# Normalised turned input of a hybrid GLA and S5 block: its tokens begin 192 bytes beyond a multiple of 256 bytes

## Chip, cores and metric

The kernel runs on one core of a Trainium2 chip. The metric is the device time of one execution in microseconds (us). The engines are named as in the profile: PE is TensorE's matrix multiplication, PEld its loading of weights, DVE is VectorE, ACT is ScalarE, POOL is GpSimd and SP is SyncE.

## The reference, cut to what matters

One decoder block is computed for 512 tokens of width 1024, with 16 meta tokens ahead of them (528 tokens in all):

```python
h = jnp.concatenate([meta, x], axis=1)          # 16 + 512 tokens
xn = rmsnorm(h, g_mix_pre)
proj = xn @ w_in                                # 1024 -> 6160 columns
# q, k, v, r, a_low, u, z_gla, z_ssm are slices of proj
y_gla = (rmsnorm(gla_chunked(q, k, v, log_a)) * silu(r)) @ w_o_gla
glu   = gelu(s5_ssm(u)) @ w_glu + b_glu
y_ssm = glu[..., :D] * sigmoid(glu[..., D:])
mixed = sigmoid(z_gla) * y_gla + sigmoid(z_ssm) * y_ssm
h = h + rmsnorm(mixed @ w_out, g_mix_post)
h = h + rmsnorm(square(relu(rmsnorm(h, g_ffn_pre) @ w_ff1)) @ w_ff2, g_ffn_post)
```

The change concerns `xn`, the operand of `xn @ w_in`.

## The kernel before

**The turned input.** `xn` is held turned: features on the 128 partitions, tokens along the free dimension, in eight feature tiles (`KT` = 8). It is held twice, as two float32r tensors that add up to it: `xh` (the rounded part, written by ScalarE in `high`, line 571) and `xl` (the rest, written by VectorE in `low`, line 576). The order along a row is the 512 tokens first and the 16 meta tokens last, `NT` = 528 numbers. The tensors are made with longer rows, `LINE + SEQ` = 64 + 512 = 576 numbers (2304 bytes, nine times 256), of which the first 528 are used (line 254).

**The products.** Each weight of `w_in` comes in tiles of 128 columns. A tile is loaded by SP (`wraw`, line 170), and split into a rounded part `whi` by ScalarE (lines 164 and 174) and a rest `wlo` by VectorE (line 179). `feat_tile` and `mm3` (lines 190 to 202) then make, for each of the eight feature tiles, three matmuls with a stationary tile of 128 x 128 and `xh` or `xl` as the moving operand:

```python
190 def mm3(ps, whi, wlo, xhi, xlo, kt, within=None):
...
195     PE.matmul(ps, whi(k), xhi(k), start=(k == 0), stop=False)
196     PE.matmul(ps, whi(k), xlo(k), start=False, stop=False)
197     last = PE.matmul(ps, wlo(k), xhi(k), start=False, stop=(k == kt - 1))
```

In the profile these are the rows `mm<-xh,whi`, `mm<-xl,whi` and `mm<-xh,wlo` of line 61, a helper that issues every matmul. A group of 24 of them makes one product. Where the meta tokens are wanted (u, v and k) a product is made in two halves, `HALVES = ((0, 256), (256, NT))`, so with moving operands of 256 and then 272 columns: three tiles of u (`u_half`, line 278), eight of v (`Head.value`, line 959) and four of k (`Head.key`, line 1010), together 15 groups of 24 of each width. Where they are not wanted (q, r and both gates z) a product takes the 512 tokens at once: four of q (line 1020), eight of r (line 1241) and sixteen of z (line 784), 28 groups of 24. The low-rank gate projection (`low_rank`, line 693) uses `xh` and `xl` with narrow weights `wa`: 32 matmuls, 32 or 16 weight columns each, half with 256 and half with 272 moving columns.

**The first tiles of u.** The first five of the eight tiles of u are made before the normalisation is known, from the raw input, in the same split form: `rh` and `rl`, with rows of the same 576 numbers of which the first 528 are used (line 462). Their matmuls have the same shapes and weights of the same kind as those of `xh` and `xl`; `raw_product` (line 582) makes them in the order of `mm3`, and `side_by_side` (line 586) makes two tiles in turn.

**Where the operands lie.** Most pools are padded: each tile takes a multiple of 256 bytes per partition (`mk`, lines 81 to 93). In the built program `xh` begins at byte 55040 of each partition and `xl` at 73472, both multiples of 256, and the `whi` and `wlo` buffers begin at multiples of 256 too. `rh` begins at 122048 and `rl` at 140480, 192 bytes beyond a multiple, since a pool that is not padded lies below theirs. With rows of 2304 bytes every feature tile of a tensor begins at the same place against 256, and the second half, 1024 bytes further on, as well.

**Order of work.** The program's order on PE, DVE and ACT is that of the code in this part (`keep_in_program_order`, lines 59 to 79; for DVE and ACT from line 521 to 1332). The products of `xh` and `xl` run from 38 us (the low-rank projection) to 350 us: u and seven tiles of z, then the heads of the GLA with the blocks of the S5 scan between the products, then the rest of z and r. Between the products stand float32 matmuls and transposes of these two parts. After 350 us neither tensor is read.

Of the kernel before, what the change touches and what calls it, by code (L numbers as in the profile page):

```python
# [10 lines left out]
F32R = mybir.dt.float32r  # L11
# [6 lines left out]
P = 128  # L18
D = 1024
KT = D // P  # L20
SEQ = 512
NM = 16
NT = NM + SEQ
# [8 lines left out]
LINE = 64  # L32
# [18 lines left out]
def hybrid_block(ctx: ExitStack, tc: tile.TileContext, io, out: bass.AP):  # L51
# [29 lines left out]
    def mk(pool, shape, dt=F32, tag=None, **kw):  # L81
        count[0] += 1
        name = f"{tag or 'x'}_{count[0]}"
        size = 1
        for n in shape[1:]:
            size *= n
        if pool not in lined or size % LINE == 0:
            return pool.tile(shape, dt, tag=tag or name, name=name, **kw)
        t = pool.tile([shape[0], -(-size // LINE) * LINE], dt, tag=tag or name, name=name, **kw)[:, :size]
        if len(shape) == 2:  # L90
            return t
        dims = " ".join("abcd"[: len(shape) - 1])
        return t.rearrange(f"p ({dims}) -> p {dims}", **dict(zip("abcd", shape[1:])))
# [4 lines left out]
    def pool(name, bufs=1, space=None, stack=None, side="left", padded=False):  # L98
        kw = {"side": side} if space is None else {"space": space}
        if space != DRAM:  # L100
            kw["reuse_waits"] = "tile"
        made = (stack or ctx).enter_context(tc.tile_pool(name=name, bufs=bufs, **kw))
        if padded:
            lined.append(made)
        return made
# [145 lines left out]
    s1 = ExitStack()  # L251
    px = pool("px", stack=s1, padded=True)
    pinned[0] = True
    xh, xl = (mk(px, [P, KT, LINE + SEQ], F32R, tag=t)[:, :, :NT] for t in ("xh", "xl"))
    w_in = io["w_in"][0]
    sg = ExitStack()
    pg = pool("pg", stack=sg)
# [1239 lines left out]
    for c4, c in enumerate(range(0, D, 256)):  # L1497
# [16 lines left out]
        for i, w in enumerate(load_w(wg[:, c : c + 256])):  # L1514
# [3 lines left out]
            t = mk(pgl, [P, SEQ], tag="ti", bufs=2)  # L1518
# [498 lines left out]
```

## Time and profile before

| | before |
|---|---|
| median of 3 runs | 869.69 us (869.55 to 870.79) |
| the profiled execution | 869.07 us, of which the span is 867.3 us |
| PE busy | 854.4 us (99%), 4952 matmuls |
| PEld busy | 727.7 us (84%) |
| DVE, ACT, POOL busy | 683.9 us (79%), 466.5 us (54%), 151.5 us (17%) |
| granted TensorE clock | 0.998 of full speed |

The span reaches from the first to the last instruction. A matmul's duration in the profile runs from its start to the end of its pipeline, so that one overlaps the next; what a matmul costs in a row of them is the time from its start to the next one's start, called its spacing here. It is read from the timeline, which gives starts to 0.01 us: from the first start of a row of n matmuls to the start of what follows, divided by n.

### The profile page before, as it was taken

The numbers are of one execution on the slowest core, as the hardware profiler recorded it, in microseconds if no ns is written. First come the engines' busy times: TensorE is split into PE (matmuls) and PEld (weight loads), VectorE is DVE, ScalarE is ACT, GpSimd is POOL, SyncE is SP. The second block draws the span as 40 slices with busy tenths as digits, with TensorE's granted clock in tenths as the row PEclk, the third lists the DMA queues.
The fourth block names the chain that finished last, engine by engine and source line by source line (L and its number), as shares of the span: only waits on it lengthen the run. The fifth ranks groups of instructions, "written<-read, shape, count | busy, mean of one in ns | idle before, by whom it ended". The sixth has DMA issues, their size and how long they took to land.

```text
span 867.3 us, 13744 instructions
## 1 busy us (share of the span) xinstructions
PE 854.4 (99%) x4952; PEld 727.7 (84%) x4952; DVE 683.9 (79%) x1263; ACT 466.5 (54%) x818; POOL 151.5 (17%) x265
## 2 busy tenths in 40 slices
PE   9999999999999999999999999999999999999996
PEld 7998889898988888888888888988888888888885
DVE  6999889979687699866888778576676677688886
ACT  7677466666764554335454466333222236885763
POOL 1123021130304223251121421021121100000001
PEclk9999999999999999999999999999999999999999
DMA  9887766655556757668788895488989967866564
GB/s 314 208 260 229 216 141 159 174 133 147 131 139 170 242 131 209 215 177 288 220 267 268 267 297 168 153 305 289 360 264 341 348 241 225 278 198 198 166 206 145
DMA packets 172492, 192.66 MB, mean 222 GB/s; under 512 B 18649, under 2 KB 127353, under 8 KB 172425
## 3 DMA queue, kind: packets, MB, share of 16 engines
q1 hardware_dynamic: 145040, 109.66, 44.1%
q0 software_dynamic: 25408, 77.93, 26.9%
q10 hardware_dynamic: 1976, 4.20, 1.7%
q8 instruction: 39, 0.64, 0.3%
q14 instruction: 29, 0.23, 0.1%
HBM read 149.52 MB, written 42.24 MB: 221 GB/s over the span
## 4 chain that ended last, share of the span: by engine, by line
PE 87%; DVE 7%; DMA 3%; ACT 2%; issue 1%; ACTq 0%; DVEq 0%; SPq 0%
PE mm L61 64%; PE sm L61 22%; DMA wraw<-in_w_ff_dram 2%; PE sm L66 1%; DMA wraw<-in_w_in_dram 1%; DVE aq L79 1%; DVE wlo L179 1%; DVE wlo L79 1%; DVE M L79 0%; ACT L79 0%; DVE bl L79 0%; DVE aq L1431 0%; DVE c L1937 0%; ACT hh L79 0%; DVE xT L79 0%
## 5 line engine op out<-in xcount | busy, mean ns | idle before, releaser
L164 ACT ACTIVATE whi<-wraw 128x1024 fp32r<-128x1024 f32 x81 | 85.8, 1060 | 182.2 <-PE mm L61 170.4
L179 DVE TENSOR_TENSOR wlo<-wraw,whi 128x1024 fp32r<-128x1024 f32 x81 | 98.9, 1222 | 77.2 <-ACT whi L164 77.1
L61 PE MATMUL mm<-xh,whi 128*128 128x512 f32 (+2 forms) x464 | 158.9, 342 | 0.0
L61 PE MATMUL mm<-xh,wlo 128*128 128x512 f32 (+2 forms) x464 | 155.9, 336 | 0.0
L61 PE MATMUL mm<-xl,whi 128*128 128x512 f32 (+2 forms) x464 | 155.6, 335 | 0.0
L61 PE MATMUL mm<-hl,whi 128*128 128x512 f32 (+1 forms) x272 | 100.8, 371 | 0.3 <-DVE hl L79 0.3
L61 PE MATMUL mm<-hh,whi 128*128 128x512 f32 (+1 forms) x272 | 100.8, 371 | 0.0
L61 PE MATMUL mm<-hh,wlo 128*128 128x512 f32 (+1 forms) x272 | 100.7, 370 | 0.0
L61 PEld LDWEIGHTS mm<-xh,whi 128*128 128x128 f32 x464 | 87.6, 189 | 9.7 <-issue 1.0
L61 PEld LDWEIGHTS mm<-xh,wlo 128*128 128x128 f32 x464 | 87.5, 189 | 9.0
L61 PEld LDWEIGHTS mm<-xl,whi 128*128 128x128 f32 x464 | 87.7, 189 | 8.4
L1854 DVE TENSOR_TENSOR wlo<-wraw,whi 128x1024 fp32r<-128x1024 f32 x56 | 68.4, 1222 | 21.9 <-ACT whi L1850 21.8
L61 PE MATMUL sm<-wlo,fh 128*128 128x512 f32 x192 | 74.8, 390 | 0.0
L61 PE MATMUL sm<-whi,fl 128*128 128x512 f32 x192 | 74.7, 389 | 0.0
L61 PE MATMUL sm<-whi,fh 128*128 128x512 f32 x192 | 74.7, 389 | 0.0
L1850 ACT ACTIVATE whi<-wraw 128x1024 fp32r<-128x1024 f32 x56 | 58.7, 1049 | 16.4 <-PE mm L61 11.7
L61 PEld LDWEIGHTS mm<-hl,whi 128*128 128x128 f32 x272 | 51.3, 188 | 9.3 <-DVE hl L79 0.6
L61 PEld LDWEIGHTS mm<-hh,whi 128*128 128x128 f32 x272 | 51.2, 188 | 8.8
L61 PEld LDWEIGHTS mm<-hh,wlo 128*128 128x128 f32 x272 | 51.2, 188 | 8.7
L164 ACT ACTIVATE fh<-f 128x512 fp32r<-128x512 f32 x48 | 30.2, 630 | 36.6 <-PE sm L61 22.8
L61 PE MATMUL mm<-gh,whi 128*128 128x512 f32 x128 | 49.8, 389 | 0.0
L61 PE MATMUL mm<-gl,whi 128*128 128x512 f32 x128 | 49.8, 389 | 0.0
(490 smaller groups left out, 1858.8 us busy)
## 6 DMA issues: line engine op xcount, KB each, us to landing
wraw<-in_w_ff_dram SPq DMA_DIRECT2D x56, 512.0 KB, 7.3
wraw<-in_w_in_dram SPq DMA_DIRECT2D x46, 512.0 KB, 4.4
w2raw<-in_w_ff_dram POOLq DMA_DIRECT2D x16, 1024.0 KB, 9.1
t2d<-w2t POOLq DMA_DIRECT2D x16, 1024.0 KB, 6.2
wraw<-t2d SPq DMA_DIRECT2D x32, 512.0 KB, 4.1
wraw<-in_w_glu_dram SPq DMA_DIRECT2D x16, 512.0 KB, 6.3
M<-kpad POOLq DMA_DIRECT2D x64, 64.0 KB, 3.7
wraw<-in_w_o_gla_dram SPq DMA_DIRECT2D x8, 512.0 KB, 6.5
```

The source lines that it names most:

```text
L61: ins = nc.tensor.matmul(*args, **kw)
L66: ins = nc.tensor.transpose(*args, **kw)
L79: return lambda *args, **kw: tc.keep_in_program_order(getattr(self.engine, name)(*args, **kw))
L164: return S.activation(dst, src, AF.Copy, scale=scale)
L179: V.tensor_sub(lo, raw, f32(hi))
L1850: halved = S.activation(bh, raw, AF.Copy)
L1854: V.tensor_sub(bl, raw, f32(bh))
```

## The change

The tokens take the last 528 numbers of the 576 instead of the first 528:

```diff
-    xh, xl = (mk(px, [P, KT, LINE + SEQ], F32R, tag=t)[:, :, :NT] for t in ("xh", "xl"))
+    xh, xl = (mk(px, [P, KT, LINE + SEQ], F32R, tag=t)[:, :, LINE - NM :] for t in ("xh", "xl"))
```

`LINE - NM` is 48 numbers, 192 bytes. The tensors keep their places and sizes, and so does everything else in memory. No instruction is added, taken away or moved on any engine: only the addresses differ at which `xh` and `xl` are written (16 casts on ACT, 8 subtractions on DVE, which also read `xh`) and read (1392 matmuls with full weights and 32 with narrow ones). A moving operand of 256 columns now begins and ends 192 bytes beyond a multiple of 256; one of 272 columns begins there and ends at a multiple (before: began at one, ended 64 bytes beyond); one of 512 columns begins and ends 192 bytes beyond. Operands of `rh` and `rl` stay as they were; for 256 and 272 columns they lie, against 256 bytes, as those of `xh` and `xl` do after the change.

## The prediction

> **What bounds the kernel now.** I read the page first, for the engine that is never idle and for the chain that ended last.
>
> ```profile
> span 867.3 us, 13744 instructions
> PE 854.4 (99%) x4952; PEld 727.7 (84%) x4952; DVE 683.9 (79%) x1263; ACT 466.5 (54%) x818; POOL 151.5 (17%) x265
> PE 87%; DVE 7%; DMA 3%; ACT 2%; issue 1%; ACTq 0%; DVEq 0%; SPq 0%
> ```
>
> PE is busy 99% of the span and makes 87% of the chain. The change touches only operands that are read between 38 and 350 us, so next I read the stretches of that part (columns: busy time and instructions of PE, PEld, DVE, ACT, POOL, then the granted clock and DMA).
>
> ```profile
> 61.00:100.00 39.00, 39.00 (x177) 32.43 (x177) 38.13 (x93) 25.36 (x34) 10.73 (x18) 1.00 0.79 231
> 100.00:262.00 162.00, 160.76 (x1320) 145.09 (x1319) 137.36 (x270) 106.02 (x208) 30.55 (x56) 1.00 0.59 148
> 262.00:350.00 88.00, 88.00 (x585) 72.04 (x584) 73.58 (x129) 43.66 (x82) 24.55 (x45) 1.00 0.69 189
> ```
>
> PE is idle for 1.2 us of 162 in the second stretch and never in the others: what PE saves or loses here, the end saves or loses, as long as DVE keeps up. DVE has 24.6 us to spare in the second stretch, 14.4 in the third, and only 0.87 us in the first. The time in question is that of the matmuls on `xh` and `xl`; of their groups I quote two per width (columns: us in all, mean ns of one).
>
> ```profile
> L61 PE MATMUL mm<-xh,whi 128*128 128x512 f32 x224 | 89.1, 398 | 0.0
> L61 PE MATMUL mm<-xl,whi 128*128 128x512 f32 x224 | 87.2, 389 | 0.0
> L61 PE MATMUL mm<-xh,whi 128*128 128x256 f32 x120 | 35.3, 294 | 0.0
> L61 PE MATMUL mm<-xl,whi 128*128 128x256 f32 x120 | 33.9, 283 | 0.0
> L61 PE MATMUL mm<-xl,whi 128*128 128x272 f32 x120 | 34.5, 287 | 0.0
> ```
>
> With three operand pairs that is 672 matmuls of 512 columns and 360 each of 256 and 272. The mean includes the pipeline's drain, so their cost is read from the timeline as spacings.
>
> **The change part by part.** It adds and moves no instruction; it can only alter how fast one runs. The writes come first.
>
> ```profile
> L79 ACT CAST xh<-xT x16: 389/412/422, 25.2 to 35.7; 128x256 fp32r<-128x256 f32 x8, 128x272 fp32r<-128x272 f32 x8
> L79 DVE TENSOR_TENSOR xl<-xT,xh x8: 679/695/712, 27.5 to 36.2; 128x512 fp32r<-128x512 f32 x4, 128x544 fp32r<-128x544 f32 x4
> L79 ACT ACTIVATE rh<-xT,g x16: 492/507/522, 3.7 to 15.1; 128x256 fp32r<-128x256 f32 x8, 128x272 fp32r<-128x272 f32 x8
> ```
>
> The nearest rows for a write 192 bytes beyond are those of `rh`, 95 ns longer than a cast of `xh`, but with a scale per partition, another operation. I take nothing for the writes, as the last one starts at 36.2 and is done by 36.9, while the first reader (the row at 38.39 below) starts 1.5 us later, behind matmuls that PE has anyway. Were each of the 16 casts 95 ns longer (1.5 us of ACT in all, beside PE's work), that cover would just be used up; nothing speaks for a gain.
>
> The reads are the matter. For 256 and 272 columns the trace of before holds the case of after, in `rh` and `rl`: the same shapes, full weights, 192 bytes beyond a multiple of 256. Rows of the timeline follow (start, duration), the first of each stretch and what follows its last; first 272 and 256 columns of `rh` and `rl`.
>
> ```profile
> 13.44 0.28 PE L61 MATMUL mm<-rh,whi 128*128 128x272 f32 x1
> ...
> 19.36 0.28 PE L61 MATMUL mm<-rh,whi 128*128 128x256 f32 x1
> ...
> 20.99 0.28 PE L61 MATMUL mm<-rl,whi 128*128 128x256 f32 x1
> ...
> 22.58 0.28 PE L61 MATMUL sm<-rh,whi 128*128 128x272 f32 x1
> ...
> 32.60 0.28 PE L61 MATMUL sm<-rh,whi 128*128 128x256 f32 x1
> ...
> 35.43 0.29 PE L61 MATMUL sm<-rh,whi 128*128 128x272 f32 x1
> ```
>
> 48 matmuls of 272 columns from 13.44 to 19.36 are spaced by 123.3 ns. 256 columns have two values: 14 in 20.99 to 22.58 by 113.6 ns, a group that began after PE had stood waiting, and 24 in 32.60 to 35.43 by 117.9 ns, a group that follows 272 columns without a pause. Now `xh` and `xl` at multiples of 256.
>
> ```profile
> 38.39 0.28 PE L61 MATMUL mm<-xh,wa 128*32 128x256 f32 x1
> ...
> 40.20 0.28 PE L61 MATMUL mm<-xh,wa 128*32 128x272 f32 x1
> ...
> 42.20 0.28 PE L61 MATMUL mm<-xh,whi 128*128 128x256 f32 x1
> ...
> 45.08 0.29 PE L61 MATMUL mm<-xh,whi 128*128 128x272 f32 x1
> ...
> 48.08 0.41 PE L61 MATMUL sm<-alow,wgr 96*128 96x256 f32 x2
> ...
> 134.72 0.47 PE L61 MATMUL mm<-xh,whi 128*128 128x256 f32 x1
> ...
> 143.37 0.38 PE L61 MATMUL mm<-xh,whi 128*128 128x256 f32 x1
> 143.59 0.28 PE L61 MATMUL mm<-xl,whi 128*128 128x256 f32 x1
> ...
> 146.33 0.29 PE L61 MATMUL mm<-xh,whi 128*128 128x272 f32 x1
> ```
>
> 24 of 256 columns from 42.20 to 45.08: 120.0 ns. 24 of 272 columns to 48.08: 125.0 ns. After a pause, 23 of 256 from 143.59 to 146.33: 119.1 ns. So at each width the shifted operand is the faster one. How many groups begin after a pause? Their first matmul is long (0.38 and 0.47 us at 143.37 and 134.72 against 0.28), which is why `xh,whi` has a mean of 294 and `xl,whi` of 283: 120 x 11 ns = 1.3 us, at 0.10 to 0.19 us each some 11 of the 15 groups.
>
> 256 columns: 11 groups x 23 x (119.1 - 113.6) = 1.4 us, and 4 groups x 24 x (120.0 - 117.9) = 0.2 us; together 1.6 us. Bounds: all 360 by 2.1 ns, 0.8 us; all by 6.4 ns (120.0 - 113.6), 2.3 us. 272 columns: 360 x (125.0 - 123.3) = 0.6 us. The 32 narrow ones: nothing, as 256 columns already run at (40.20 - 38.39) / 16 = 113.1 ns there.
>
> 512 columns have no row with a shifted start. Their spacing now:
>
> ```profile
> 62.22 0.39 PE L61 MATMUL mm<-xh,whi 128*128 128x512 f32 x1
> ...
> 66.30 0.39 PE L61 MATMUL mm<-xh,whi 128*128 128x512 f32 x1
> ...
> 119.75 0.39 PE L61 MATMUL mm<-xl,whi 128*128 128x512 f32 x1
> ...
> 121.83 0.39 PE L61 MATMUL mm<-xl,whi 128*128 128x512 f32 x1
> ```
>
> 18 from 62.22 to 66.30: 226.7 ns; 9 after a pause, to 121.83: 231.1 ns. Bounds: a gain as large as the 256 columns' (6.4 ns, so 672 x 6.4 = 4.3 us), and a loss as large (4.3 us). I take no change of the steady spacing, by the row of narrow weights: 256 columns that nothing disturbs take 113.1, twice that is 226.2, so the steady 512 columns look undisturbed already. What their weight loads cost them seems to show only after a pause, 4.4 ns for some 9 matmuls; the shifted 256 columns lack that phase (113.6 at once). If the shift spared it in all 28 groups, that were 28 x 9 x 4.4 = 1.1 us; I take 0.4.
>
> The sum: 1.6 + 0.6 + 0.4 = 2.6 us, all of it on PE. Of this, 2.2 us fall where 256 and 272 columns run, for the most part between 100 and 262 us, where DVE has 24.6 us to spare, and it cannot run out there. The profiled execution took 869.07 us, so 866.5; the median of the runs is 0.62 us above it, so on that scale 869.7 - 2.6 = 867.1 us.
>
> **The rivals.** *The 512 columns gain as well.* If the disturbance is a fixed price of a start at a multiple of 256, they too get 6.4 ns: 2.2 + 4.3 = 6.5 us, 863.2 us. For it: 120.0 and 226.7 lie above 256 and 512 columns by the same 13.3 ns, if a column takes 1 / 2.4 ns (an estimate from the difference: 106.7 ns for 256 columns more). Against it: twice 113.1 is 226.2. Between 61 and 100 us DVE's 0.87 us would cap what some 170 matmuls could give there (1.1 us), which changes little.
>
> *The 512 columns lose.* In a shifted row they run over nine blocks of 256 bytes in place of eight, and the phase against the weight loads, which now settles after a pause, may never settle: 256 columns show both values at the same shift, and the worse one (117.9) held for a whole group. Staying at 231.1 costs 672 x 4.4 = 3.0 us, net 0.8: 870.5. A whole step of 6.4 ns costs 4.3, net 2.1: 871.8. The point from which it decides: over 2.2 us / 672 = 3.3 ns more per matmul the kernel is slower than before. For it speaks only that such phases exist; against it, that in both measured widths the shift is better.
>
> *Nothing changes.* The spacings of `rh` would be those of their part of the program (other PSUM banks, other neighbours), and the start of an operand would not matter: 869.7. For it: 113.1 occurs at a multiple of 256 too, with narrow weights, so the start is not the cause alone. Against it: `rh` groups in the order and with the weights of the `xh` groups still differ from them by 2 to 6 ns. The Trainium skill would side with it: "TensorE: Matmul & The Clock Gate", Part 2: What happens when you issue a matmul, says that PE has two independent read ports, one for the moving operand and one for weights, and that loading weights takes no read bandwidth from the running matmul; by that rule no start can be worse against the weights. The trace disagrees as far as the rows at 38.39 and 42.20 go: same operand, same width, narrow against full weights, 113.1 against 120.0 ns.
>
> **How the numbers follow.** My forecast has 0.45, the 512 columns' gain 0.22, their loss 0.15, nothing 0.18. A measurement of this kernel can tell 0.2%, 1.7 us, from no change. The forecast's own range is 865.9 to 868.5; about five sixths of its weight lie beyond 1.7 us. Faster: 0.22 + 0.38 = 0.60. Within 0.2%: 0.07 of the forecast, 0.18 and a third of the losses, 0.05, so 0.30. Slower: 0.10. The range goes from 862.9, which holds the second case, to 870.6, which holds no change and the milder loss.
>
> **What would show it.** In the profile after, groups of 256 columns after a pause spaced by 113 to 114 ns, the others by 118; 272 columns by 123.3; 512 columns by 226.7, with at most fewer at 231 after a pause. DVE and ACT keep their busy times, and the part after 350 us is the same, only earlier by 2 to 3 us. Wrong it is if 512 columns are spaced by anything but 226 to 227 ns, or if 256 columns stay at 119 to 120.

## The result and the profile after

The changed kernel takes 870.93 us (median of 22 runs, 870.02 to 872.05) against 869.62 us (22 runs, 868.47 to 871.32) for the kernel before, run beside it: a ratio of 1.0015, 95% interval 1.0008 to 1.0021. It is 1.3 us slower, where 2.6 us less had been forecast. The profiled execution of the changed kernel took 870.58 us.

The page of the kernel after: the span, the engines, the chain.

```profile
span 868.9 us, 13744 instructions
PE 856.0 (99%) x4952; PEld 726.2 (84%) x4952; DVE 684.0 (79%) x1263; ACT 465.9 (54%) x818; POOL 151.7 (17%) x265
PE 85%; DVE 9%; DMA 3%; ACT 2%; issue 1%; ACTq 0%; DVEq 0%; SPq 0%
```

The span is 1.6 us longer and PE is busy for 1.6 us more with the same 4952 matmuls. No other engine's busy time has grown by more than 0.2 us. So the time went into PE's own work, and the stretches say where (here only PE's columns: the stretch, its length, PE busy and instructions, clock, DMA share, GB/s).

```profile
61.00:100.00 39.00, 39.00 (x169) 1.00 0.78 231
100.00:262.00 162.00, 160.42 (x1327) 1.00 0.59 148
```

Between 61 and 100 us, where nearly everything has 512 columns, PE is busy without a break in both kernels, and gets 169 matmuls done in place of 177. Between 100 and 262 us, where 256 and 272 columns are common, it gets 1327 done in place of 1320, though it stands idle for 1.58 us in place of 1.24. Something has become dearer and something cheaper, by width. The groups of the kernel after confirm it (us in all, mean ns of one):

```profile
L61 PE MATMUL mm<-xh,whi 128*128 128x512 f32 x224 | 90.1, 402 | 0.0
L61 PE MATMUL mm<-xh,whi 128*128 128x256 f32 x120 | 34.7, 289 | 0.0
L61 PE MATMUL mm<-xl,whi 128*128 128x256 f32 x120 | 33.2, 277 | 0.0
L61 PE MATMUL mm<-xl,whi 128*128 128x272 f32 x120 | 34.4, 287 | 0.0
```

512 columns of `xh`: 89.1 us before, 90.1 now. 256 columns: 35.3 and 33.9 before, 34.7 and 33.2 now. The spacings are read from the timeline of the kernel after, at the places whose rows the prediction showed (start, duration; the first of a stretch, and the first of the next).

```profile
42.61 0.29 PE L61 MATMUL mm<-xh,whi 128*128 128x256 f32 x1
...
45.35 0.28 PE L61 MATMUL mm<-xh,whi 128*128 128x272 f32 x1
...
48.31 0.66 PE L61 MATMUL sm<-alow,wgr 96*128 96x256 f32 x4
...
60.71 0.39 PE L61 MATMUL mm<-xh,whi 128*128 128x512 f32 x1
...
99.91 0.28 PE L61 MATMUL mm<-xh,whi 128*128 128x256 f32 x1
...
120.28 0.39 PE L61 MATMUL mm<-xl,whi 128*128 128x512 f32 x1
...
122.14 0.39 PE L61 MATMUL mm<-xh,whi 128*128 128x512 f32 x1
...
144.21 0.28 PE L61 MATMUL mm<-xl,whi 128*128 128x256 f32 x1
...
146.82 0.28 PE L61 MATMUL mm<-xh,whi 128*128 128x272 f32 x1
```

24 of 256 columns from 42.61 to 45.35: 114.2 ns (120.0 before), of which all but the first two or three are at 113.3. 23 after a pause, from 144.21 to 146.82: 113.5 ns (119.1 before). 24 of 272 columns to 48.31: 123.3 ns (125.0). 168 of 512 columns from 60.71 to 99.91: **233.3 ns, where they had 226.7**. Just behind a pause, eight from 120.28: 232.5 ns (231.1).

Taken over every matmul on `xh` and `xl` with full weights (from each start to the next in the trace), the 672 of 512 columns take 3.74 us more (155.66 before, 159.40 after), the 360 of 256 columns 1.85 us less (44.47, 42.62), the 360 of 272 columns 0.66 us less (45.87, 45.21). That is 1.23 us more. From the first of these products to the last it is 306.2 us before and 307.8 after, 1.6 more; nearly all of the rest is PE's longer standing between 100 and 262 us (0.34 us). The view of the waits in that stretch (what waited, for what, us in all, times, longest) has two of it, which were 0.5 and 0.4 us before:

```profile
PE sm L66 <- DVE e_gk L79: 0.7, 1, 0.7
PE sm L66 <- ACT on L1091: 0.6, 1, 0.6
```

Outside these products little differs: what stands ahead of them takes 0.4 us more and what follows them 0.5 us less (518.9 us before, 518.4 after). Neither is an effect of the change that could be told from chance, since kernels with the same work behind them took 518.3 to 520.7 us for it (experiments 4, 5, 11 and 12).

### The profile page after: what moved, and what is told of

The parts are those of the page before. It is cut to its first block, busy times and chain, and to the rows that moved or that the text cites. A ratio compares the mean times of both kernels' runs of the same rounds, so it can differ in the third digit from the quotient of the medians.

```text
span 868.9 us, 13744 instructions
## 1 busy us (share of the span) xinstructions
PE 856.0 (99%) x4952; PEld 726.2 (84%) x4952; DVE 684.0 (79%) x1263; ACT 465.9 (54%) x818; POOL 151.7 (17%) x265
## 4 chain that ended last, share of the span: by engine, by line
PE 85%; DVE 9%; DMA 3%; ACT 2%; issue 1%; ACTq 0%; DVEq 0%; SPq 0%
PE mm L61 62%; PE sm L61 21%; DMA wraw<-in_w_ff_dram 2%; PE sm L66 1%; DMA wraw<-in_w_in_dram 1%; DVE wlo L179 1%; DVE wlo L79 1%; DVE aq L79 1%; DVE M L79 1%; ACT L79 0%; DVE xT L79 0%; DVE bl L79 0%; DVE aq L1431 0%; DVE c L1937 0%; ACT hh L79 0%
```

## The experiments

Two theories stood at the start. **A**: the cost depends on where the moving operand begins against a multiple of 256 bytes, for each width in its own way. **B**: it depends on where the moving operand begins *relative to the weights* that PE loads at the same time (whose rows of 512 bytes begin at a multiple of 256 in this kernel). The change moves one against the other, so both explain the result; they differ on what moving the weights does.

One length recurs below: the *xh part*, from the start of the first product of `xh` with full weights to the start of the last, in the profiled execution. It is 306.2 us before and 307.8 after, and it holds what the theories speak of, without what happens to the kernel elsewhere. It repeats closely: where the products lie as before (experiments 6 and 9), it came to 306.23 and 306.25 us again.

**1. All starts and widths by themselves.** The kernel before, with 864 extra matmuls after the gates' weights are loaded: the order of the real products, into a bank whose sums nobody reads, for starts of 0, 64, 128 and 192 bytes and three widths, with full weights and with 16 columns of weights.

```diff
+    def probe(start, n, times=2, shift=None, narrow=False):
+        ps = bank("mm")
+        for _ in range(times):
+            for k in range(KT):
+                for w, x in ((0, xhw), (0, xlw), (1, xhw)):
...
+                    PE.matmul(ps[:, :n], whole[:, a : a + P], x[:, k, start : start + n], start=True, stop=True)
+    for start in (0, 16, 32, 48):
+        for n in (512, 256, 272):
+            probe(start, n)
```

> The kernel before with 480 pairs' worth of extra matmuls after the low-rank projection, whose sums nobody reads: rows of 48 float32r matmuls of 512, 256 and 272 columns that start 0, 64, 128 and 192 bytes beyond a multiple of 256, with full weights, then rows of 24 with 16 weight columns. Theory A (the moving operand alone: every start that isn't a multiple of 256 makes 512 columns run over nine blocks of 256 bytes and pay one step of 6.7 ns): 512 columns at 226.7 ns from start 0 and 233.3 from 64, 128 and 192, with full and narrow weights alike. Theory B (the moving operand against the weights that are loaded meanwhile): with full weights 226.7 and 233.3 at starts 0 and 192, the other starts anywhere between 220 and 233, but with narrow weights one spacing for all starts, 226.7. Both: 256 columns with full weights at 120.0 from start 0 and 113.3 from 192; 272 at 125 and 123.5.

The timeline of this kernel: 512 and 256 columns with full weights at 0 bytes, the same at 192 bytes, and 24 of 512 columns with narrow weights.

```profile
42.28 0.40 PE L61 MATMUL mm<-xh,whi 128*128 128x512 f32 x1
...
53.21 0.28 PE L61 MATMUL mm<-xh,whi 128*128 128x256 f32 x1
...
58.97 0.29 PE L61 MATMUL mm<-xh,whi 128*128 128x272 f32 x1
...
110.42 0.39 PE L61 MATMUL mm<-xh,whi 128*128 128x512 f32 x1
...
121.62 0.28 PE L61 MATMUL mm<-xh,whi 128*128 128x256 f32 x1
...
127.06 0.28 PE L61 MATMUL mm<-xh,whi 128*128 128x272 f32 x1
...
132.99 0.39 PE L61 MATMUL mm<-xh,wa 128*16 128x512 f32 x1
...
138.32 0.51 PE L61 MATMUL mm<-xh,wa 128*16 128x512 f32 x2
```

48 matmuls each: 512 columns at 0 bytes (53.21 - 42.28) / 48 = 227.7 ns, at 192 bytes 233.3; 256 columns 120.0 and 113.3. The narrow row is the telling one: 23 matmuls of 512 columns from 132.99 to 138.32 at 231.7 ns, with 16 weight columns in place of 128. All of them, steady (mean over the second half of a stretch, ns):

| start, bytes | 0 | 64 | 128 | 192 |
|---|---|---|---|---|
| 512 columns, full weights | 226.65 | 228.7 | 232.3 | 233.2 |
| 256 columns, full weights | 120.0 | 113.35 | 118.6 | 113.3 |
| 272 columns, full weights | 125.4 | 126.65 | 126.7 | 123.4 |
| 512 columns, narrow | 231.8 | 231.9 | 231.6 | 232.0 |
| 256 columns, narrow | 113.3 | 113.4 | 113.4 | 113.4 |

What follows: both of the changed kernel's spacings come out of the start alone, without the rest of the kernel. And with narrow weights the start makes no difference, at 231.8 for 512 columns, which neither theory expected (both had 226.7 for narrow weights at 0): twice 113.3 is not what 512 columns take there. At 0 bytes full weights make 512 columns *faster* than narrow ones do, by 5 ns, and 256 columns slower, by 6.7.

**2. The weights moved too.** The same, with the weights read from 0, 64, 128 or 192 bytes beyond a multiple of 256 (they are then columns of two neighbouring blocks), for operands at 0 and 192; then operands at 16, 32, 96 and 160 bytes.

```diff
+    for shift in (0, 16, 32, 48):
+        for start in (0, 48):
+            for n in (512, 256):
+                probe(start, n, 2, shift=shift)
```

> The kernel before with extra matmuls whose sums nobody reads, rows of 42 with the stationary tile read 0, 64, 128 and 192 bytes beyond a multiple of 256, each with the moving operand at start 0 and at 192 bytes, 512 and 256 columns; then rows of 48 with starts 16, 32, 96 and 160 bytes and weights at 0. Theory A: the weights' place changes nothing, 226.7 and 120.0 at start 0, 233.3 and 113.3 at 192, in all four rows. Theory B: what counts is the difference of the two places, so weights at 64 with start 0 (difference 192) give 233.3 and 113.3, and weights at 192 with start 192 give 226.7 and 120.0.

The timeline: 42 matmuls in each stretch; weights at 0 with the operand at 0, weights at 0 with it at 192, weights at 64 with it at 0, and, last, weights and operand both at 192.

```profile
42.26 0.40 PE L61 MATMUL mm<-xh,whi 128*128 128x512 f32 x1
...
51.83 0.28 PE L61 MATMUL mm<-xh,whi 128*128 128x256 f32 x1
...
56.86 0.40 PE L61 MATMUL mm<-xh,whi 128*128 128x512 f32 x1
...
66.67 0.28 PE L61 MATMUL mm<-xh,whi 128*128 128x256 f32 x1
...
71.44 0.39 PE L61 MATMUL mm<-xh,whi 128*128 128x512 f32 x1
...
81.23 0.28 PE L61 MATMUL mm<-xh,whi 128*128 128x256 f32 x1
...
145.07 0.40 PE L61 MATMUL mm<-xh,whi 128*128 128x512 f32 x1
...
154.62 0.28 PE L61 MATMUL mm<-xh,whi 128*128 128x256 f32 x1
```

512 columns: 227.9 ns from 42.26, 233.6 from 56.86, 233.1 from 71.44, and 227.4 from 145.07, where the operand is at 192 as in the changed kernel, but the weights are too. Steady:

| weights at, bytes | 0 | 64 | 128 | 192 |
|---|---|---|---|---|
| 512 columns at 0 | 226.65 | 233.35 | 233.35 | 233.35 |
| 512 columns at 192 | 233.35 | 231.95 | 229.05 | 226.65 |
| 256 columns at 0 | 120.0 | 117.8 | 118.7 | 117.75 |
| 256 columns at 192 | 113.3 | 120.1 | 117.8 | 120.0 |

What follows: A falls. Moving the weights alone takes 512 columns from 226.65 to 233.35, and moving them along with the operand brings both widths back to the values of before. B holds as far as this: equal places (both at 0, both at 192) give 226.65 and 120.0. It doesn't hold as a rule of the difference alone: operand 64 bytes beyond the weights gave 228.7 in experiment 1 (weights at 0) and 233.35 here (weights at 192). For 256 columns it was 113.35 there and 117.75 here, but those two values also turn up at one and the same place (experiment 4), so they decide nothing. That 256 bytes is the measure, and not 512, shows within each product: feature tiles lie 2304 bytes apart and weight tiles 512, so that modulo 512 every second feature tile lies 256 bytes otherwise against its weights, and yet the steady spacings do not alternate (227, 227, 226 ns throughout). Operands at 16, 32, 96 and 160 bytes, weights at 0: 231.7 to 234.3 for 512 columns, 116.6 to 119.9 for 256; no start has the best of both.

**3. How many columns of weights.** All weights at a multiple of 256 bytes, 16 to 128 columns of them.

```diff
+                    PE.matmul(ps[:m, :n], f0[w][:, k, :m], x[:, k, start : start + n], start=True, stop=True)
...
+    for m in (16, 32, 64, 96, 128):
+        for start in (0, 48):
+            for n in (512, 256):
+                probe(start, n, m)
```

> The kernel before with extra matmuls whose sums nobody reads: rows of 48 with 16, 32, 64, 96 and 128 weight columns, all read from multiples of 256 bytes, each with the moving operand at start 0 and at 192 bytes, 512 and 256 columns. If full weights that begin together with the operand help 512 columns, 226.7 ns at start 0 comes with 128 columns alone, and fewer give about 232 at both starts; if weights that begin at a multiple of 256 help whatever their number, 226.7 at start 0 in all five rows. 256 columns: 120.0 with 128 weight columns at start 0, 113.3 with 96 or fewer, if the load of the next weights is what they wait for.

The timeline: 512 columns at 0 with 16 weight columns; then with 128 weight columns 512 and 256 columns at 0, and 512 at 192.

```profile
42.56 0.40 PE L61 MATMUL mm<-xh,whi 128*16 128x512 f32 x1
...
53.69 0.28 PE L61 MATMUL mm<-xh,whi 128*16 128x256 f32 x1
...
175.42 0.39 PE L61 MATMUL mm<-xh,whi 128*128 128x512 f32 x1
...
186.31 0.28 PE L61 MATMUL mm<-xh,whi 128*128 128x256 f32 x1
...
192.07 0.40 PE L61 MATMUL mm<-xh,whi 128*128 128x512 f32 x1
...
203.28 0.28 PE L61 MATMUL mm<-xh,whi 128*128 128x256 f32 x1
```

48 of 512 columns: 231.9 ns with 16 weight columns, 226.9 with 128 at the same place, 233.5 with 128 at 192 bytes. 256 columns with 128 weight columns at 0: (192.07 - 186.31) / 48 = 120.0. Steady, operand at 0 and at 192:

| weight columns | 16 | 32 | 64 | 96 | 128 |
|---|---|---|---|---|---|
| 512 columns at 0 / 192 | 231.7 / 231.6 | 231.8 / 231.8 | 229.8 / 232.4 | 230.0 / 228.3 | 226.65 / 233.3 |
| 256 columns at 0 / 192 | 113.35 / 113.35 | 113.35 / 113.35 | 113.3 / 119.1 | 115.9 / 117.2 | 120.0 / 113.3 |

What follows: up to 32 weight columns the place doesn't matter, and the two widths have 231.8 and 113.35. From 64 on it does, and it takes either sign: with 128, 226.65 is a help to 512 columns, 120.0 a hindrance to 256 columns, both from weights read at the operand's own place. In between no simple rule shows: 64 and 96 columns are neither as narrow nor as full ones, and 256 columns with 96, expected at 113.3, took 115.9.

**4. The changed kernel with its 512 columns cut in two.** If 256 columns are the better for the shift, let everything have 256.

```diff
+        if c1 - c0 == SEQ and any(xh is t for t in twice):
+            for c in (c0, c0 + 256):
+                last = feat_tile(w, xh, xl, c, c + 256, ps[:, c - c0 : c - c0 + 256])
+            return last
```

> The kernel after, with each product of 512 columns on the turned input made as two products of 256 columns, one after the other, in the two halves of the same bank: 1344 matmuls of 256 for 672 of 512. If the loss sits in the 512 columns alone (233.3 against 226.7 ns) and 256 shifted columns cost 113.5 in any place, 672 x (233.3 - 2 x 113.5) = 4.2 us less than after: 866.7 us, 2.9 less than before. If a half of 256 that follows another without a pause falls to 117.9 ns, 672 x 2.5 = 1.7 us more than after, 872.6. DVE has under 1 us to spare between 61 and 100 us and may hold back a little.

869.98 us (11 runs), the kernel before in the same job 869.19 (15 runs): ratio 1.0012, interval 1.0003 to 1.0021. It lies between the two times that were expected, some 3 us from either. The timeline, where 168 halved pairs and the 24 matmuls of the product behind them run in one stretch of 360:

```profile
60.16 0.28 PE L61 MATMUL mm<-xh,whi 128*128 128x256 f32 x1
...
102.56 0.29 PE L61 MATMUL mm<-xh,whi 128*128 128x272 f32 x1
```

360 matmuls at 117.8 ns, not 113.5: a pair takes 235.6, more than 512 columns in either kernel. In other stretches the same halves ran at 113.3. At a shift of 192 bytes 256 columns thus have two values, 113.3 and 117.8, and a stretch that has settled at one, after some eight matmuls, keeps it to its end.

**5. The kernel before with its 512 columns cut in two**, the same edit on it.

> The kernel before, with the same division of its 512 columns into two halves of 256, which start at multiples of 256 bytes. If spacing on PE is the whole price, 672 x (2 x 120.0 - 226.7) = 8.9 us slower than before, 878.5 us. If DVE, DMA or the weight loads set the pace there, less.

One run: 878.33 us, near the 878.5 expected, in part by luck. The spacing is 120.0 ns nearly everywhere, and the products with full weights take 8.0 us more (246.0 to 254.0 us from start to start), not 8.9; the xh part is 313.6 us, 7.4 longer, as PE stands 0.6 us less in it. The other 1.9 us came later, between the last product of `gh` and the first of `hh` (42.7 us before, 44.6 here), where one run can't tell cause from chance. In the xh part, cutting a product costs nothing beyond the spacing of its halves.

**6. Wider weight buffers, nothing moved (a control).** To move the weights, their buffers need 256 bytes more room in each partition, paid for here with one of four `qi` buffers of the stage after 400 us.

```diff
+    def placed(tag, at):
+        t = mk(wp, [P, KT * P + LINE], F32R, tag=tag, bufs=3)
+        return t[:, at : at + KT * P].rearrange("p (k n) -> p k n", n=P)
...
-            q = mk(pgl, [P, SEQ], tag="qi", bufs=4)
+            q = mk(pgl, [P, SEQ], tag="qi", bufs=3)
```

> A control: the kernel before, with 256 bytes more for each of the six whi and wlo buffers (nothing is put there), which moves all that lies above by 1536 bytes, six times 256; to make room, the pool tile qi of the GLU stage has three buffers in place of four. Both theories: all spacings as before (120.0, 125.4, 226.7 ns), and 869.2 us, unless the fourth qi buffer was needed; what it costs then is taken off the next two.

877.11 us (6 runs) against 868.94: ratio 1.0099, interval 1.0079 to 1.0120. The xh part is 306.2 us, as before. A later stretch:

```profile
403.00:520.00 117.00, 111.16 (x481) 1.00 0.81 248
```

PE stands idle for 5.84 us there (0.23 before). The missing fourth buffer is the likely cause; no run takes it away without widening the others. So experiments 7 and 8 are compared with this kernel, and by their xh part.

**7. The changed kernel with its weights moved along**, 192 bytes, where the products have 512 columns (`q`, `r`, `z`), and left at 0 where they have 256 and 272 (`u`, `v`, `k`).

```diff
-            dense.append((cols("w_in", C_Q + h * P), self.query))
+            dense.append((cols("w_in", C_Q + h * P), self.query, 48))
...
```

> The control with the turned input 192 bytes beyond, as in the kernel after, and with the weights of the 512-column products (q, r, z) written 192 bytes beyond as well; those of the 256 and 272 columns (u, v, k) stay at multiples of 256. Theory B (the difference of the two places): 512 columns at 226.7 ns as before, 256 at 113.3 to 114.3, 272 at 123.6, so 360 x (119.6 - 114.3) + 360 x (125.4 - 123.6) = 2.6 us less than the control, 866.6 us. Theory A (the moving operand's place alone): 512 columns at 233.3, 1.2 us more than the control, 870.4.

874.2 us (6 runs), ratio to before 1.0072, interval 1.0053 to 1.0091; 2.9 us less than the control. Its 512 columns between 61 and 99 us:

```profile
61.05 0.39 PE L61 MATMUL mm<-xh,whi 128*128 128x512 f32 x1
...
99.17 0.28 PE L61 MATMUL mm<-xh,whi 128*128 128x256 f32 x1
```

168 at 226.9 ns, with the operand at 192 bytes as in the changed kernel, where they took 233.3. Over all products with full weights, 512 columns take 155.65 us, exactly the control's, 256 columns 1.49 us less and 272 columns 0.64 less: 2.1 us. The xh part is 304.7 us, 1.5 less than the control's; PE stands 0.6 us longer in it. The rest of the 2.9 us lies outside the xh part, where the control's own runs differ by 7 us (874.55 to 881.64), and isn't credited to the weights. The 256 columns gain 1.49 and not 1.85 since they have 113.3 in some stretches and 117.8 in others, 115.3 in the mean.

**8. The kernel before with the weights moved alone**: 64 bytes for `q`, `r`, `z`, the operand left at 0.

```diff
-            dense.append((cols("w_in", C_Q + h * P), self.query))
+            dense.append((cols("w_in", C_Q + h * P), self.query, 16))
...
```

> The control with the turned input at a multiple of 256, as in the kernel before, and only the weights of the 512-column products written 64 bytes beyond (the difference of moving operand to weights is 192 against 256, as in the kernel after). Theory B: 512 columns at 233.3 ns, 3.7 us more than the control (672 x 6.7, less what they pay after pauses anyway), 872.9 us; 256 and 272 columns unchanged. Theory A: all as in the control, 869.2 us.

881.69 us (4 runs), ratio 1.0146, interval 1.0133 to 1.0159; 4.6 us more than the control, 3.4 of them in the xh part (309.6 us). Over all products with full weights, 512 columns take 3.76 us more than the control's, and 256 and 272 columns the same as there.

```profile
61.16 0.40 PE L61 MATMUL mm<-xh,whi 128*128 128x512 f32 x1
...
100.37 0.28 PE L61 MATMUL mm<-xh,whi 128*128 128x256 f32 x1
```

168 at 233.4 ns: the loss of the changed kernel, made without touching `xh` or `xl`. This is the run that speaks plainest against A.

**9 and 10. Room for the weights from another pool.** Experiments 6 and 7 again, with the weight buffers in a pool (a region of on-chip memory from which tiles are given out) of their own that is wide only during the xh part, and four `qi` buffers.

```diff
+    placed.pool = pool("ws", stack=s1, padded=True), LINE
...
+    placed.pool = pool("ws2", padded=True), 0
```

> The control to it: the same two pools, nothing put beyond a multiple of 256. Both theories: the spacings and the time of the kernel before, 869.2 us; what the pools cost by themselves shows here.

> The version that the runs so far point to: the turned input 192 bytes beyond, the weights of the 512-column products 192 bytes beyond as well, those of the 256 and 272 columns at multiples of 256; the wider whi and wlo buffers stand in a pool of their own that is closed with the turned input's, so that the fourth qi buffer stays. Theory B: 256 columns at 114.3 to 115.3 ns, 272 at 123.6, 512 at 226.7, so 360 x (119.6 - 114.8) + 360 x (125.4 - 123.6) = 2.4 us less than before, 866.7 us, faster than both kernels. If the pool's closing makes the first weights of the next part wait, some of it is lost there.

With nothing moved 876.01 us (5 runs), ratio to before 1.0073, interval 1.0059 to 1.0086; with weights and operand moved 874.72 us (5 runs), ratio 1.0055, interval 1.0041 to 1.0069. The xh part again shows the gain, 306.2 and 304.7 us. The room again costs more, elsewhere; the control's stretch in which the pool is reopened:

```profile
346.00:403.00 57.00, 53.86 (x328) 1.00 0.67 204
```

PE, which never stands idle there before, does so for 3.14 us up to 403, and for 4.3 us up to 520 (0.2 before). As a version to keep, moving the weights failed twice, by what the room costs.

**11. A start of 64 bytes**, where experiment 1 had 113.35 for 256 columns and 228.7 for 512.

```diff
-    xh, xl = (mk(px, [P, KT, LINE + SEQ], F32R, tag=t)[:, :, LINE - NM :] for t in ("xh", "xl"))
+    xh, xl = (mk(px, [P, KT, LINE + SEQ], F32R, tag=t)[:, :, 16 : 16 + NT] for t in ("xh", "xl"))
```

> The kernel before with its tokens 64 bytes beyond a multiple of 256 in place of 192. By the rows of extra matmuls at that start: 512 columns at 228.7 ns, 672 x 2.0 = 1.4 us more; 256 at 113.4, 360 x 6.2 = 2.2 us less; 272 at 126.6, 360 x 1.2 = 0.4 us more: net 0.4 us less than before, 868.8 us, if these rows hold in the kernel, where products follow pauses and other shapes. If only a start at a multiple of 256 suits 512 columns, 233.3 there: 2.8 us more, 872.

870.42 us (11 runs), ratio 1.0014, interval 1.0006 to 1.0023; missed by 1.6 us. 512 columns came as in experiment 1 (228.9 ns between 61 and 99 us) and 272 at 126.6, but 256 columns, in 13 of 15 groups, at 117.7, the higher of their two values, and so took 0.8 us less where 2.2 had been expected. The xh part is 307.0 us, 0.8 longer than before; the other 0.7 us lies outside it.

**12. Both places at once.** The tokens lie at a multiple of 256 bytes as in the kernel before, so 512 columns begin there. The row's spare 48 numbers take a second copy of the first 48 tokens, and `u`, `v` and `k` are cut as 48 to 303 and 304 to 575, so that 256 and 272 columns begin 192 bytes beyond; what they give is copied to its place in two pieces.

```diff
+ROUND = ((AGAIN, AGAIN + 256), (AGAIN + 256, AGAIN + NT))
...
+    S.copy(xhw[:, :, NT:], f32(xhw)[:, :, :AGAIN])
+    S.copy(xlw[:, :, NT:], f32(xlw)[:, :, :AGAIN])
...
-            for a, b in HALVES:
+            for q, (a, b) in enumerate(ROUND):
...
-                feat_tile(w, xh, xl, a, b, ps)
-                self.taken = S.copy(vt[:, a:b], ps)
+                feat_tile(w, xhw, xlw, a, b, ps)
+                self.taken = rounded(vt, q, ps)
```

> The kernel before, tokens at a multiple of 256 bytes, with the first 48 tokens written once more into the 48 numbers that each row has to spare (two casts on ACT), and with the halves of u, v and k cut as columns 48 to 303 and 304 to 575: these begin 192 bytes beyond a multiple of 256, those of 512 columns at one. All weights stay at multiples of 256. The second half's sums are taken out of PSUM in two or three pieces, 18 short ACT copies more. If each width keeps the spacing of its place: 512 columns at 226.7 ns, 256 at 114.3 to 115.3, 272 at 123.6, so 2.4 us less than before, 866.8 us; that is the gain that the prediction saw, without the loss. If the short copies hold PE back by 0.1 us each, 868.6.

**867.8 us** (11 runs, 867.18 to 868.62) against 869.19 (15 runs): ratio 0.9984, interval 0.9975 to 0.9993. It is the only one of these kernels that beats the kernel before, by 1.4 us; 1.0 us of the expected gain is missing. Its page and its timeline:

```profile
span 865.5 us, 13762 instructions
```

```profile
42.33 0.28 PE L63 MATMUL mm<-xh,whi 128*128 128x256 f32 x1
...
45.09 0.28 PE L63 MATMUL mm<-xh,whi 128*128 128x272 f32 x1
...
60.45 0.39 PE L63 MATMUL mm<-xh,whi 128*128 128x512 f32 x1
...
98.54 0.28 PE L63 MATMUL mm<-xh,whi 128*128 128x256 f32 x1
```

256 columns at 115.0 ns from 42.33, and 512 at 226.7 from 60.45: each width at its better place. Over all products with full weights 512 columns take 155.64 us (155.66 before), 256 columns 1.56 less, 272 columns 0.65 less: 2.2 us. The xh part is only 1.4 shorter, 304.8 us; its waits show why.

```profile
PE sm L68 <- DVE e_gk L81: 0.9, 1, 0.9
PE sm L68 <- ACT on L1105: 0.8, 1, 0.8
```

The two waits have grown from 0.5 and 0.4 us by 0.8 in all: part of what PE gains ahead of them, it stands there. The 256 columns' second value costs some more (the 24 from 98.54 on run at 117.8; the mean over all is 115.1).

## Why the prediction was wrong

*The writes: right.* The casts of `xh` take 410 ns in the median (412 before), the differences `xl` 703 (695), and none of it is waited for. The first product of the xh part begins 0.4 us later (42.6), but that start lies anywhere from 41.9 to 42.9 in these profiles, among kernels whose work up to there is the same.

*256 columns: right in sign, a little low.* Forecast 1.6 us less, came 1.85. The 4 groups without a pause were to run at 117.9 and ran at 113.3, while 2 of the 11 behind a pause (from 113.26 and 196.84 us) were to run at 113.6 and ran at 117.8. The `rh` rows were a good guide to the two values, a poor one to which comes where, and that the sum came so near is partly luck.

*272 columns: right*, 0.6 forecast, 0.66 found.

*"It cannot run out there": wrong, by 0.3 us.* The prediction put the gains of 256 and 272 columns on the path whole, as DVE has 24.6 us to spare between 100 and 262 us. But a stretch's spare time is no promise for a single wait: PE waits for DVE's `e_gk` and ACT's `on` once each, and these two waits grow as PE gets there sooner, by 0.4 us in the changed kernel and by 0.8 in experiment 12.

*512 columns: this step failed.* The prediction took "no change of the steady spacing, by the row of narrow weights: 256 columns that nothing disturbs take 113.1, twice that is 226.2, so the steady 512 columns look undisturbed already". The doubling was the mistake. Experiment 3 shows 512 columns with 16 weight columns at 231.7, and 231.6 at the other start: by the prediction's own yardstick, narrow weights, that is what nothing disturbs. The 226.7 of the kernel before was a help that came from weights read at the same place against 256 bytes, and the change took the help away and left a small hindrance (233.35): a term of 0, less 0.4 for the phase behind a pause, was 3.74 us more.

*The phase behind a pause: misread.* The 231.1 ns behind a pause were taken as a loss that the loads cause. They are near the 231.7 that 512 columns take with narrow weights, so they look like the time without the help; the 226.7 sets in up to ten matmuls later (235, 234, 236, 224, 231, 235, 229, 232 and 231 ns are the first of experiment 1, then 226.65 throughout). In the shifted kernel no such settling comes, so there was no 0.4 us to save.

*The rivals.* "The 512 columns lose", with a whole step of 6.4 ns and 871.8 us, is what happened, at 6.7 ns (226.65 to 233.35) in the steady stretches; its break-even of 3.3 ns per matmul was passed. 672 x 6.7 were 4.5 us; it came to 3.74 since the matmuls behind pauses already had 231. Of the two reasons given for it the nine blocks of 256 bytes fall: with narrow weights the shifted 512 columns run over the same nine and lose nothing (231.6 against 231.7). A phase against the weight loads that never settles comes nearer, though what holds in the shifted kernel is 233.35 and not the 231.1 that stand behind a pause. The rival had a chance of 0.15, on the ground that in both measured widths the shift was better: two widths at which the weights hinder were taken to speak for a third, at which they help.

*Nothing changes*, the rival that the Trainium skill sided with, is wrong too. "TensorE: Matmul & The Clock Gate", Part 2: What happens when you issue a matmul, has the two read ports independent, and says that loading weights takes no read bandwidth from the running matmul. By that the weights' place could do nothing. Experiment 8 moves the weights alone, with the moving operand untouched, and 512 columns go from 226.7 to 233.4; experiment 2 has both values, and back. For this type of operand the measurement decides: the place of the weights does change the running matmuls' spacing. Whether that is by read bandwidth no run here shows.

*What stays open.* That the two operands' places act together is shown, not what in the chip makes it so. Equal places are the only case with a simple rule; the difference between places is not enough (228.7 and 233.35 for the same difference), and the number of weight columns counts. Why 256 columns at one and the same place run at 113.3 in one stretch and at 117.8 in another isn't settled; a pause ahead doesn't decide it (in experiment 4 two stretches that begin behind a pause have 113.4 from 106.21 and 117.7 from 113.19).

## What to carry to other kernels

A spacing below another is not proof that the other is disturbed: before one width's row stands for another's, measure that width with narrow weights, since here the same neighbour helped 512 columns by 5 ns and hindered 256 by 6.7. When an operand is moved within its rows, count each width by itself and multiply by its number of matmuls: 672 small losses beat 720 small gains. And where each width has its own best place, a few numbers written twice can give both (1.4 us here), while room for moving a buffer can cost more than it brings (8.2 us in one control, 877.11 against 868.94, and 6.5 in the other, 876.01 against 869.51).

## What the hardware showed that was not expected

The place of the weights against the place of the moving operand, modulo 256 bytes, changes the spacing of float32r matmuls by up to 3% at 512 columns (226.65 to 233.35 ns) and 6% at 256 (113.3 to 120.0), in opposite senses; with 32 or fewer weight columns it changes nothing (231.8 and 113.35). Full weights can make a matmul faster than narrow ones do (226.65 against 231.7). A steady spacing may need up to ten matmuls to set in, and at some places there are two, each of which lasts for a whole stretch (113.3 and 117.8).
